# Conditioning rows of a transformer layer: added one transfer step later, in written order, from three buffers; later shift and scale columns by one-column products

## The chip, the cores and the metric

The kernel runs on one core of a Trainium2 chip. The metric is the time on the device in microseconds, the median of several runs. TensorE (PE) does the matrix products, VectorE (DVE) and ScalarE (ACT) the elementwise work, GpSimd (POOL) a little of it, and SyncE (SP) issues nearly all transfers into on-chip memory, in order. Each engine works through its own queue of instructions in a fixed order and waits, where it must, for another engine or a transfer.

## The reference

One layer, 256 tokens of 2048 features, all in fp32. A vector `c` gives nine vectors of 2048 by one large matrix, `w_ada` (2048 x 18432, 151 MB): a shift, a scale and a gate for each of three parts.

```python
ada = (silu(c) @ w_ada + b_ada)
sh1, sc1, g1, sh2, sc2, g2, sh3, sc3, g3 = split(ada, 9)
h = swiglu(layernorm(x) * (1 + sc1) + sh1, ffn1_w_in, ffn1_w_out)
x = layernorm(ALPHA * x + 0.5 * (1 + g1) * h, ln1_g, ln1_b)
h = token_mixer(layernorm(x) * (1 + sc2) + sh2, ...)      # 8 attention heads, 4 mLSTM heads, w_out
x = layernorm(ALPHA * x + (1 + g2) * h, ln2_g, ln2_b)
h = swiglu(layernorm(x) * (1 + sc3) + sh3, ffn2_w_in, ffn2_w_out)
x = layernorm(ALPHA * x + 0.5 * (1 + g3) * h, ln3_g, ln3_b)
```

## The kernel before

**Products.** Each fp32 operand is split into a rounded high part and the rest, and a product is three matmuls: high by high (L355), low by high (L356), high by low (L357). Weights come in tiles of 1 MB by SP's queue (`raw_...`, three buffers); ScalarE writes the high part (`hi_...`, L145), VectorE subtracts it to get the low part (`lo_...`, L146). In names, `s` and `f1i` are FFN1's input product, `f1o` its output product, `mo`, `fv`, `mv` parts of the mixer's input product, `mxo` its output product, `fh` and `gf` (`gu`) the beginning of FFN2's input product, `f2i` the rest of it, `f2o` its output product. `hT` is a hidden row of the FFN, `hh` and `hl` its two parts, `o_f` and `o_mx` the output sums.

**The conditioning vectors.** They are not computed on TensorE as a product with a single row. A block of 128 rows of `w_ada` by 1024 columns (512 KB, `ar...`) is transferred, and VectorE multiplies it by one scalar for each partition and adds it to a sum (`acc`, L158 for the first, L160 for the other fifteen of a sum). The 128 partitions are then added up by a product with ones:
- The first shift and scale (`first_ada`, L691) take products of one column each: 128 columns of the sum as weights, a column of ones as moving operand. What comes out already lies one feature to a partition, as `scsh` needs it.
- All later sums are split, and a matrix of ones gives the sum in all partitions (`bc`, L173). For a gate that is the form in which it is used (L213). For a shift or scale the diagonal has to be picked out: a multiplication with the identity (`dg`, L191), a reduction (L193), and the bias (L195).

**The order of this work.** Everything after the first pair is one generator, `ada_queue`. The loops over weight tiles call `pump(n)`, which goes on by `n` steps (rates `R_F` to `R_B` for the stages); one step issues a row's transfer and its add, in two buffers. `need(n)` drains the queue up to part `n` where its result is used:

```python
    def need(n):
        while parts_done[0] < n and next(ada_left["g"], 0) != 0:
            owed[0] = 0
```

The framework's scheduler may move instructions on an engine within what the data allow; so a written add can end up earlier or later on VectorE than its neighbours in the code. `out_proj` keeps unfinished additions to the residual in a list and lets `catch_up(n)` write `n` of them for each weight tile.

Of the kernel before, what the change touches and what calls it, by code (L numbers as in the profile page):

```python
# [47 lines left out]
def layer_kernel(  # L48
# [41 lines left out]
    tri = ap.tile([P, 2 * P], F32, tag="ahi", name="tri")  # L90
# [9 lines left out]
    crow = ap.tile([KD, P], F32, tag="alo", name="crow")  # L100
# [15 lines left out]
    def load_bcol():  # L116
        brow = ap.tile([72, 2, P], F32, tag="ahi", name="brow")
# [38 lines left out]
    def ada_acc(acc, raw, k):  # L156
        if k == 0:
            V.tensor_scalar_mul(acc, raw, csil[:, k:k + 1])  # L158
        else:
            V.scalar_tensor_tensor(out=acc, in0=raw, scalar=csil[:, k:k + 1], in1=acc,  # L160
                                   op0=ALU.mult, op1=ALU.add)


    def ada_split(acc, tag):
        ahi = ap.tile([P, 512], F32R, tag="ahi", name=f"ahi{tag}")
        alo = ap.tile([P, 512], F32R, tag="alo", name=f"alo{tag}")
        split(acc, ahi, alo)
        return ahi, alo

    def ada_sum(parts, tag):  # L170
        bc = aux_tile(f"bc{tag}")
        for i in range(2):
            PE.matmul(bc, onesr, parts[i], start=i == 0, stop=i == 1)  # L173
        return bc

    def ada_pair(v, js):
        for j in js:
            src = pair_cols(v, j)
            acc = ap.tile([P, 2, 512], F32, tag="acc", name=f"acc{v}_{j}")
            for k in range(KD):  # L180
                raw = ap.tile([P, 2, 512], F32, tag="araw", bufs=2, name=f"ar{v}_{j}_{k}")
                SP.dma_start(raw, src[k * P:(k + 1) * P])
                ada_acc(acc, raw, k)
                yield
            for i in range(2):
                parts = ada_split(acc[:, i, :], f"{v}_{j}_{i}")
                for _ in range(2):
                    yield PAUSE
                bc = ada_sum(parts, f"{v}_{j}_{i}")
                dg = ap.tile([P, 4, P], F32, tag="alo", name=f"dg{v}_{j}_{i}")  # L190
                V.tensor_tensor(out=dg, in0=bc.rearrange("p (a b) -> p a b", b=P),  # L191
                                in1=ident.unsqueeze(1).to_broadcast([P, 4, P]), op=ALU.mult)
                V.tensor_reduce(out=scsh[:, v + i, j * 4:(j + 1) * 4], in_=dg, axis=AX.X, op=ALU.add)  # L193
            cs = scsh[:, v:v + 2, j * 4:(j + 1) * 4]
            V.tensor_tensor(out=cs, in0=cs, in1=bcol[:, v:v + 2, j * 4:(j + 1) * 4], op=ALU.add)  # L195

    def ada_gate(v, s):
        for j in range(2):
            c0 = v * D + j * 1024
            acc = ap.tile([P, 1024], F32, tag="acc", name=f"acc{v}_{j}")  # L200
            for k in range(KD):
                raw = ap.tile([P, 1024], F32, tag="araw", bufs=2, name=f"ar{v}_{j}_{k}")
                SP.dma_start(raw, w_ada[0, k * P:(k + 1) * P, c0:c0 + 1024])
                ada_acc(acc, raw, k)
                yield
            G_.dma_start(gate[:, j * 1024:(j + 1) * 1024], b_ada[0:1, c0:c0 + 1024].to_broadcast([P, 1024]))
            for i in range(2):
                parts = ada_split(acc[:, i * 512:(i + 1) * 512], f"{v}_{j}_{i}")
                for _ in range(2):
                    yield PAUSE  # L210
                bc = ada_sum(parts, f"{v}_{j}_{i}")
                gs = gate[:, j * 1024 + i * 512:j * 1024 + (i + 1) * 512]
                V.scalar_tensor_tensor(out=gs, in0=bc, scalar=1.0, in1=gs, op0=ALU.add, op1=ALU.add)  # L213
                if s != 1.0:
                    V.tensor_scalar_mul(gs, gs, s)

    ada_left = {}
    PAUSE = 1

    def ada_queue(*parts):  # L220
        def gen():
            for p in parts:
                yield from p
                parts_done[0] += 1
                yield PAUSE
        ada_left["g"] = gen()

    parts_done = [0]
    owed = [0]

    def pump(n):
        owed[0] += n
        while owed[0] >= 1:
            if next(ada_left["g"], 0) is PAUSE:
                break
            owed[0] -= 1


    def need(n):
        while parts_done[0] < n and next(ada_left["g"], 0) != 0:  # L240
            owed[0] = 0


# [141 lines left out]
    def out_proj(w, rows, nk, tag, npump, finish, before=None, turn=0, nheld=3, spare=None):  # L385
# [11 lines left out]
        for width in (1024, 512, 512):  # L397
# [40 lines left out]
            for i in range(nu):  # L438
# [19 lines left out]
                if not lastg and i == nu - 1:  # L458

                    late += [add_up(a, bs=(b,)) for b in range(nb) for a in range(2)]  # L460
                    products(0, held)
                    catch_up(2)
                    products(1, held)
                else:
                    catch_up(2)
                if not lastg or i < nu - 4:
                    npump()
            if lastg:
                catch_up(99)
                finish(last_products, add_up, st)  # L470
            else:
                col += width
# [50 lines left out]
    def boundary(products, add_up, st, lgb, v, tag, xT, entry, nk):  # L523
# [3 lines left out]
        sq = ap.tile([P, 1024], F32, tag="araw", bufs=2, name=f"sq_{tag}")  # L527
# [83 lines left out]
    def cols_1024(raws, xs, split_, load, ps, xT, npump, u0, u1):  # L611
# [6 lines left out]
        for u in range(u0 + len(raws), u1):  # L618
            for k, hi, lo in split_.get(u) or load(u):
# [18 lines left out]
    R_F, R_IN, R_OUT, R_MX, R_A, R_B = 1.25, 1.2, 1, 1.42, .9, .6  # L638
# [14 lines left out]
    def first_ada(j, ws=iter(())):  # L653
# [5 lines left out]
        for kk in range(8):  # L659
            if kk % 3 == 2:  # L660
                raws = []
                for h in range(2):
                    k = 2 * kk + h
                    raw = ap.tile([P, 2, 512], F32, tag="araw", bufs=2, name=f"ar0_{j}_{k}")
# [106 lines left out]
    with tc.manual_schedule(engines={mybir.EngineType.DVE, mybir.EngineType.Activation}):  # L771
        next(fa)
    ada_queue(ada_gate(2, 0.5), ada_pair(3, range(4)), ada_pair(6, range(2)), ada_gate(5, 1.0),
              ada_pair(6, range(2, 3)), ada_pair(6, range(3, 4)), ada_gate(8, 0.5))
    for j in range(4):
        fa = first_ada(j + 1) if j < 3 else load_mixer_smalls()
        for i in range(NS):
            first_in(j, i, ws if i + j == 0 else first_w(j, i))
            for _ in range(i not in (4, 9, 11)):
                next(fa, 0)  # L780
            if j == 3 and i > 2:
# [9 lines left out]
    need(1)  # L791
# [14 lines left out]
    def finish1(products, add_up, st):  # L806
        need(2)
# [376 lines left out]

    def before(k):
        until([f"row{i}" for i in (k, k + 1)])
        if k == 2:
            need(4)
# [80 lines left out]
    for j in range(2, 10):  # L1269
# [12 lines left out]
    for _ in mb:  # L1282
        pass
    gups = {(a, g): mm_tile(f"gf{g}{a}") for a in range(2) for g in range(2)}
    cols_1024([], {}, {}, gu_load, gups, xT, at(R_B), 4, 8)
# [23 lines left out]
    need(7)  # L1309
# [42 lines left out]
```

## Time and profile before

| | us |
|---|---|
| three runs | 1976.5, 1969.3, 1975.67; median 1975.67 |
| the profiled execution | 1967.35 |
| its span from first to last instruction | 1965.6 |
| TensorE busy | 1900.2 |
| VectorE busy | 1486.1 |
| ScalarE busy | 944.3 |
| mean granted clock of TensorE | 0.995 |

The profiled execution is 1.75 us longer than its span. Times inside it are counted from the span's start. In a row of a timeline stand the start, the duration, the engine, the line, the operation with its output and inputs, and in brackets how long the engine idled before it and what ended that. In a row of waits stand the total, the number and the longest. Matmuls overlap, so their cost is the distance from start to start, and the printed duration is longer. In a row of windows the columns behind the engines' busy times are the granted clock, the share of the transfer engines and GB/s.

### The profile page before, as it was taken

To read this page: it belongs to the slowest core of one execution; us is meant where nothing else is said; L and a number is where in the kernel's file an instruction comes from. 1 tells how busy PE (TensorE), PEld (TensorE's weight loads), DVE (VectorE), ACT (ScalarE), POOL (GpSimd) and SP (SyncE) were. 2 spreads that over 40 slices of the span, in tenths; PEclk is the share of its full clock that TensorE was granted. 3 is DMA by queue.
4 is the path that set the end of the run, shared out by engine and by line. 5 is a ranking of instruction groups with operands and counts; after the bars stand their busy time and mean duration, and the time that the engine had idled before them with its cause. 6 is when DMAs were issued, how large, how long until landed. Compare 5 with 4: busy or idle time off the path is not lost.

```text
span 1965.6 us, 32416 instructions
## 1 busy us (share of the span) xinstructions
PE 1900.2 (97%) x13201; PEld 1736.7 (88%) x13201; DVE 1486.1 (76%) x1827; ACT 944.3 (48%) x1328; POOL 19.6 (1%) x34
## 2 busy tenths in 40 slices
PE   3999999999999999999999999999999999999997
PEld 3999999999988888588999876899999999988886
DVE  7788888777778898678888687778756645555776
ACT  2544354443444554645755543555444444444552
POOL 0000000000000000000000000000000000000000
PEclk9999999999999999999999999999999999999998
DMA  9999878989989785589888784898757855655552
GB/s 335 333 326 315 309 234 294 310 291 303 317 297 310 269 292 199 174 302 298 268 299 287 266 276 147 293 297 296 260 194 254 278 194 187 236 191 192 193 193 86
DMA packets 301822, 510.91 MB, mean 260 GB/s; under 512 B 10819, under 2 KB 158691, under 8 KB 300649
## 3 DMA queue, kind: packets, MB, share of 16 engines
q1 hardware_dynamic: 300808, 505.70, 76.5%
q0 software_dynamic: 864, 3.15, 0.5%
q8 instruction: 103, 1.69, 0.4%
q14 instruction: 47, 0.38, 0.1%
HBM read 506.71 MB, written 2.10 MB: 259 GB/s over the span
## 4 chain that ended last, share of the span: by engine, by line
PE 77%; DMA 9%; DVE 9%; ACT 2%; issue 2%; POOL 0%; SPq 0%; DVEq 0%; ACTq 0%; POOLq 0%
PE o_f L355 8%; PE o_f L357 8%; PE o_f L356 8%; PE gu_f L355 7%; PE gu_f L357 7%; PE gu_f L356 7%; DMA ar<-in_w_ada_dram 5%; PE s L357 3%; PE s L355 3%; PE s L356 3%; DVE acc L160 2%; PE pr_f L356 2%; PE pr_f L355 2%; PE pr_f L357 2%; PE fs L355 1%
## 5 line engine op out<-in xcount | busy, mean ns | idle before, releaser
L160 DVE SCALAR_TENSOR_TENSOR acc<-ar,csil,acc 128x1024 f32<-128x1024 f32 x242 | 307.7, 1272 | 106.7 <-DMA ar<-in_w_ada_dram 105.3
L355 PE MATMUL s<-xhi_f,hi_s 128*128 128x256 f32 x768 | 213.8, 279 | 0.8 <-ACT hi_s L145 0.6
L357 PE MATMUL s<-xhi_f,lo_s 128*128 128x256 f32 x768 | 213.1, 278 | 0.6 <-DVE lo_s L146 0.5
L356 PE MATMUL s<-xlo_f,hi_s 128*128 128x256 f32 x768 | 213.4, 278 | 0.0
L357 PE MATMUL gu_f<-xhi_f,lo_f2i 128*128 128x256 f32 x768 | 212.0, 276 | 0.0
L355 PE MATMUL gu_f<-xhi_f,hi_f2i 128*128 128x256 f32 x768 | 212.0, 276 | 0.0
L356 PE MATMUL gu_f<-xlo_f,hi_f2i 128*128 128x256 f32 x768 | 212.0, 276 | 0.0
L146 DVE TENSOR_TENSOR lo_f2i<-raw_f2i,hi_f2i 128x1024 fp32r<-128x1024 f32 x96 | 116.8, 1223 | 89.5 <-ACT hi_f2i L145 89.5
L355 PE MATMUL gu_f<-xhi_f,hi_f1i 128*128 128x256 f32 x640 | 176.8, 276 | 0.2 <-DVE hT L740 0.2
L357 PE MATMUL gu_f<-xhi_f,lo_f1i 128*128 128x256 f32 x640 | 176.7, 276 | 0.0
L356 PE MATMUL gu_f<-xlo_f,hi_f1i 128*128 128x256 f32 x640 | 176.7, 276 | 0.0
L145 ACT CAST hi_f2i<-raw_f2i 128x1024 fp32r<-128x1024 f32 x96 | 100.4, 1049 | 133.7 <-PE gu_f L356 112.4
L355 PEld LDWEIGHTS s<-xhi_f,hi_s 128*128 128x128 f32 x768 | 145.1, 189 | 1.1 <-ACT hi_s L145 0.7
L357 PEld LDWEIGHTS s<-xhi_f,lo_s 128*128 128x128 f32 x768 | 144.9, 189 | 1.1 <-DVE lo_s L146 1.1
L356 PEld LDWEIGHTS s<-xlo_f,hi_s 128*128 128x128 f32 x768 | 145.2, 189 | 0.3 <-DVE xlo_f L297 0.3
L356 PEld LDWEIGHTS gu_f<-xlo_f,hi_f2i 128*128 128x128 f32 x768 | 144.1, 188 | 0.2
L355 PEld LDWEIGHTS gu_f<-xhi_f,hi_f2i 128*128 128x128 f32 x768 | 144.1, 188 | 0.2
L145 ACT CAST hi_s<-raw_s 128x1024 fp32r<-128x1024 f32 x96 | 97.3, 1050 | 97.5 <-DMA raw_s<-in_ffn_w_in_dram 56.6
L357 PEld LDWEIGHTS gu_f<-xhi_f,lo_f2i 128*128 128x128 f32 x768 | 144.1, 188 | 0.0
L146 DVE TENSOR_TENSOR lo_f2o<-raw_f2o,hi_f2o 128x1024 fp32r<-128x1024 f32 x88 | 107.7, 1224 | 44.9 <-ACT hi_f2o L145 44.8
L355 PE MATMUL o_f<-hi_f2o,hh 128*128 128x512 f32 (+1 forms) x368 | 139.4, 379 | 0.0
L357 PE MATMUL o_f<-hi_f2o,hl 128*128 128x512 f32 (+1 forms) x368 | 138.7, 377 | 0.0
(451 smaller groups left out, 5342.0 us busy)
## 6 DMA issues: line engine op xcount, KB each, us to landing
ar<-in_w_ada_dram SPq DMA_DIRECT2D x288, 512.0 KB, 5.7
raw_s<-in_ffn_w_in_dram SPq DMA_DIRECT2D x48, 1024.0 KB, 6.0
raw_f2i<-in_ffn_w_in_dram SPq DMA_DIRECT2D x48, 1024.0 KB, 5.1
raw_f1o<-in_ffn_w_out_dram SPq DMA_DIRECT2D x44, 1024.0 KB, 6.9
raw_f2o<-in_ffn_w_out_dram SPq DMA_DIRECT2D x44, 1024.0 KB, 5.1
raw_f1i<-in_ffn_w_in_dram SPq DMA_DIRECT2D x40, 1024.0 KB, 7.7
raw_mxo<-in_w_out_dram SPq DMA_DIRECT2D x16, 1024.0 KB, 6.8
raw_fh<-in_ffn_w_in_dram SPq DMA_DIRECT2D x16, 1024.0 KB, 7.5
```

The source lines that it names most:

```text
L145: S.copy(hi, src)
L146: V.tensor_tensor(out=lo, in0=src, in1=hi.bitcast(F32), op=ALU.subtract)
L160: V.scalar_tensor_tensor(out=acc, in0=raw, scalar=csil[:, k:k + 1], in1=acc, op0=ALU.mult, op1=ALU.add)
L355: PE.matmul(o, ah, bh, start=start, stop=False)
L356: PE.matmul(o, ah, bl, start=False, stop=False)
L357: return PE.matmul(o, al, bh, start=False, stop=stop)
```

## The change

- **Rows.** Transfers are issued by `ada_rows` into three buffers and noted in `landing`. The next call of `pump` or `need` writes their adds first (`add_landed`); at most two rows wait at a time. `keep_in_program_order` forbids the scheduler to move an add past its neighbours in the written order. At most three steps can be owed.
- **Sums.** What a sum needs after its last row (`columns`) is a generator of its own, which goes on by one step at each `pump`, beside the next sum's rows. A later shift and scale takes eight one-column products of the unsplit sum (L192) and one addition of the bias; the split, `bc`, `dg` and the reduction are gone. A gate's sum is split in one piece of 1024 columns instead of two of 512.
- **Places.** `R_OUT` is 1.1 instead of 1, `R_A` 1.2 instead of 0.9. `need` counts smaller parts and stands elsewhere: in the mixer's output product before units 8 and 12, in `fh` at step 7. The modulation of chunk 3 for FFN2, with its `need`, moves from `fh` (step 9) into `gf` between two weight tiles (`last_features`). `out_proj` catches up three pieces instead of two for the wide columns and none in the last group before its end. The first stage issues weights before it goes on with the first ada sums.

The core of the diff:

```diff
-    def ada_pair(v, js):
-        for j in js:
-            ...
-            acc = ap.tile([P, 2, 512], F32, tag="acc", name=f"acc{v}_{j}")
-            for k in range(KD):
-                raw = ap.tile([P, 2, 512], F32, tag="araw", bufs=2, name=f"ar{v}_{j}_{k}")
-                SP.dma_start(raw, src[k * P:(k + 1) * P])
-                ada_acc(acc, raw, k)
-                yield
-            for i in range(2):
-                parts = ada_split(acc[:, i, :], f"{v}_{j}_{i}")
-                for _ in range(2):
-                    yield PAUSE
-                bc = ada_sum(parts, f"{v}_{j}_{i}")
-                dg = ap.tile([P, 4, P], F32, tag="alo", name=f"dg{v}_{j}_{i}")
-                V.tensor_tensor(out=dg, in0=bc..., in1=ident..., op=ALU.mult)
-                V.tensor_reduce(out=scsh[:, v + i, j * 4:(j + 1) * 4], in_=dg, axis=AX.X, op=ALU.add)
+    def ada_acc(acc, raw, k):
+        ...
+        tc.keep_in_program_order(ins)
+
+    def ada_rows(acc, src, tag):
+        for k in range(KD):
+            raw = ap.tile([P, 1024], F32, tag="araw", bufs=3, name=f"ar{tag}_{k}")
+            SP.dma_start(raw.rearrange("p (v n) -> p v n", v=2), src[k * P:(k + 1) * P])
+            landing.append((acc, raw, k))
+            yield PAUSE if k == KD - 1 else None
+
+    def ada_pair(v, j):
+        acc = ap.tile([P, 1024], F32, tag="acc", name=f"acc{tag}")
+        yield from ada_rows(acc, pair_cols(v, j), tag)
+
+        def columns():
+            yield
+            cp = aux_tile(f"ac{tag}")[:, :8]
+            for i in range(8):
+                PE.matmul(cp[:, i:i + 1], acc[:, i * P:(i + 1) * P], ones[:, 0:1], start=True, stop=True)
+            yield
+            V.tensor_tensor(out=scsh[:, v:v + 2, js], in0=cp..., in1=bcol[:, v:v + 2, js], op=ALU.add)
+        yield columns()
+
     def pump(n):
-        owed[0] += n
-        while owed[0] >= 1:
-            if next(ada_left["g"], 0) is PAUSE:
-                break
-            owed[0] -= 1
+        add_landed()
+        end_columns()
+        ada["owed"] = min(ada["owed"] + n, 3)
+        while ada["owed"] >= 1 and len(landing) < 2 and not (ada["ends"] and ada["beside"]):
+            got = next_row()
+            ...
@@ out_proj
-                else:
+                elif nu > 4:
                     catch_up(2)
+                elif not lastg:
+                    catch_up(3)
...
-    R_F, R_IN, R_OUT, R_MX, R_A, R_B = 1.25, 1.2, 1, 1.42, .9, .6
+    R_F, R_IN, R_OUT, R_MX, R_A, R_B = 1.25, 1.2, 1.1, 1.42, 1.2, .6
...
-        if j in (7, 9):
-            need(5 if j == 7 else 6)
-            mb = modulate_both(6, 2 if j == 7 else 3, mr2, xT)
+        if j == 7:
+            need(11)
+            mb = modulate_both(6, 2, mr2, xT)
...
+    def last_features(u):
+        if u == 5:
+            need(12)
+            mb.append(modulate_both(6, 3, mr2, xT))
```

Three places show how the instructions stand now.

VectorE, the beginning of FFN1's output product; `acc_1` is a sum of the second shift and scale (its rows `ar_1_...`), `hT` the last rows that this product needs first. Before:

```order
L160 SCALAR_TENSOR_TENSOR acc_1_5912<-ar_1_8_6119,csil,acc_1_5912 128x1024
L160 SCALAR_TENSOR_TENSOR acc_1_5912<-ar_1_9_6122,csil,acc_1_5912 128x1024
L146 TENSOR_TENSOR lo_f1o_11_6271<-raw_f1o_1_6252,hi_f1o_11_6270 128x1024
L146 TENSOR_TENSOR lo_f1o_20_6296<-raw_f1o_2_6293,hi_f1o_20_6295 128x1024
L160 SCALAR_TENSOR_TENSOR acc_1_5912<-ar_1_10_6183,csil,acc_1_5912 128x1024
L380 TENSOR_TENSOR hT_3_111<-sg_f_0_6186,gu_f_0_5937 128x256
L160 SCALAR_TENSOR_TENSOR acc_1_5912<-ar_1_11_6245,csil,acc_1_5912 128x1024
L380 TENSOR_TENSOR hT_3_111<-sg_f_1_6189,gu_f_1_5938 128x256
```

After the change, the same place:

```order
L160 SCALAR_TENSOR_TENSOR acc_1_5709<-ar_1_10_6223,csil,acc_1_5709 128x1024
L146 TENSOR_TENSOR lo_f1o_20_6273<-raw_f1o_2_6270,hi_f1o_20_6272 128x1024
L402 TENSOR_TENSOR hT_3_111<-sg_f_0_6162,gu_f_0_5913 128x256
L146 TENSOR_TENSOR lo_f1o_21_6289<-raw_f1o_2_6270,hi_f1o_21_6288 128x1024
L402 TENSOR_TENSOR hT_3_111<-sg_f_1_6165,gu_f_1_5914 128x256
L146 TENSOR_TENSOR hl_6226<-hT_0_108,hh_6225 128x512
L146 TENSOR_TENSOR hl_6267<-hT_0_108,hh_6266 128x512
L160 SCALAR_TENSOR_TENSOR acc_1_5709<-ar_1_11_6264,csil,acc_1_5709 128x1024
```

The add of row 10 went ahead of `lo_f1o_20`, and that of row 11 behind both `hT` and two `hl`.

VectorE, the last part of the mixer's output product: low parts of its weights (`lo_mxo`) and the pieces that add the product to the residual (`o_mx` times gate, `res`, and its statistics `st_mx`). Before:

```order
L146 TENSOR_TENSOR lo_mxo_20_12252<-raw_mxo_2_12249,hi_mxo_20_12251 128x1024
L435 BN_STATS st_mx_11638<-res 128x6
L146 TENSOR_TENSOR lo_mxo_21_12256<-raw_mxo_2_12249,hi_mxo_21_12255 128x1024
L431 TENSOR_TENSOR o_mx_12057<-o_mx_12057,gate 128x512
L146 TENSOR_TENSOR lo_mxo_30_12264<-raw_mxo_3_12261,hi_mxo_30_12263 128x1024
L433 SCALAR_TENSOR_TENSOR res<-res,o_mx_12057 128x512
L146 TENSOR_TENSOR lo_mxo_31_12268<-raw_mxo_3_12261,hi_mxo_31_12267 128x1024
L435 BN_STATS st_mx_11637<-res 128x6
L431 TENSOR_TENSOR o_mx_12058<-o_mx_12058,gate 128x512
L146 TENSOR_TENSOR lo_mxo_00_12276<-raw_mxo_0_12273,hi_mxo_00_12275 128x1024
```

After the change:

```order
L146 TENSOR_TENSOR lo_mxo_20_12174<-raw_mxo_2_12171,hi_mxo_20_12173 128x1024
L453 TENSOR_TENSOR o_mx_11977<-o_mx_11977,gate 128x512
L160 SCALAR_TENSOR_TENSOR acc_2_11516<-ar_2_15_12100,csil,acc_2_11516 128x1024
L146 TENSOR_TENSOR lo_mxo_21_12178<-raw_mxo_2_12171,hi_mxo_21_12177 128x1024
L146 TENSOR_TENSOR lo_mxo_30_12184<-raw_mxo_3_12181,hi_mxo_30_12183 128x1024
L146 TENSOR_TENSOR lo_mxo_31_12188<-raw_mxo_3_12181,hi_mxo_31_12187 128x1024
L146 TENSOR_TENSOR lo_mxo_00_12194<-raw_mxo_0_12191,hi_mxo_00_12193 128x1024
L146 TENSOR_TENSOR lo_mxo_01_12198<-raw_mxo_0_12191,hi_mxo_01_12197 128x1024
L455 SCALAR_TENSOR_TENSOR res<-res,o_mx_11977 128x512
L453 TENSOR_TENSOR o_mx_11978<-o_mx_11978,gate 128x512
```

The low parts stand together now and the pieces of the residual follow them, while the last add of the sum `acc_2`, which lay ahead of this place before, stands among them.

SP, the transfers of the mixer's input weights `fv` and `mv` with ada rows between them. Before:

```order
L339 DMA raw_fv_0_8709<-in_w_in_dram 128x4x520
L182 DMA ar_0_2_8576<-in_w_ada_dram 128x2x512
L182 DMA ar_0_3_8579<-in_w_ada_dram 128x2x512
L339 DMA raw_fv_1_8778<-in_w_in_dram 128x4x520
L182 DMA ar_0_4_8616<-in_w_ada_dram 128x2x512
L182 DMA ar_0_5_8653<-in_w_ada_dram 128x2x512
L339 DMA raw_fv_2_8847<-in_w_in_dram 128x4x520
```

After the change:

```order
L361 DMA raw_fv_0_8673<-in_w_in_dram 128x4x520
L168 DMA ar_0_9_8544<-in_w_ada_dram 128x2x512
L168 DMA ar_0_10_8582<-in_w_ada_dram 128x2x512
L361 DMA raw_fv_1_8743<-in_w_in_dram 128x4x520
L168 DMA ar_0_11_8619<-in_w_ada_dram 128x2x512
L168 DMA ar_0_12_8621<-in_w_ada_dram 128x2x512
L168 DMA ar_0_13_8741<-in_w_ada_dram 128x2x512
L361 DMA raw_fv_2_8812<-in_w_in_dram 128x4x520
```

Three rows instead of two stand ahead of `raw_fv_2`; the queue goes on with two rows, `raw_fv_3`, one row, `raw_mv_0` and `raw_mv_1`, where two rows stood ahead of each before. Later, five rows stand in one piece between `raw_mxo_0` and `raw_mxo_1`.

More of the change, by code (lines that the diff above doesn't have):

```diff
@@ L157, in ada_acc @@
         if k == 0:
-            V.tensor_scalar_mul(acc, raw, csil[:, k:k + 1])
+            ins = V.tensor_scalar_mul(acc, raw, csil[:, k:k + 1])
         else:
[L160 to L168, printed above, removed]
@@ L217, in layer_kernel @@
[L217 to L229, printed above, removed]
-    def pump(n):
-        owed[0] += n
-        while owed[0] >= 1:
-            if next(ada_left["g"], 0) is PAUSE:
-                break
-            owed[0] -= 1
-    def need(n):
-        while parts_done[0] < n and next(ada_left["g"], 0) != 0:
-            owed[0] = 0
+            ins = V.scalar_tensor_tensor(out=acc, in0=raw, scalar=csil[:, k:k + 1], in1=acc,
+                                         op0=ALU.mult, op1=ALU.add)
@@ new lines, in layer_kernel, with add_landed, end_columns, next_row @@
+    PAUSE, STARTED, ENDED = 1, 2, 3
+    ada = {"left": [], "rows": None, "ends": None, "beside": 0, "done": 0, "owed": 0}
+    landing = []
+    def add_landed():
+        while landing:
+            ada_acc(*landing.pop(0))
+    def end_columns():
+        if ada["ends"] and next(ada["ends"], 0) == 0:
+            ada["ends"] = None
+            ada["done"] += 1
+    def next_row():
+        if not ada["rows"]:
+            if not ada["left"]:
+                return ENDED
+            ada["rows"] = ada["left"].pop(0)
+        got = next(ada["rows"])
+        if got in (None, PAUSE):
+            return got
+        ada.update(ends=got, rows=None, beside=0)
+        next(got)
+        return STARTED
@@ L790, in layer_kernel @@
     gap(lnp, 320, "gap_h")
-    need(1)
+    need(2)
     W = w_in[0]
@@ L1308, in layer_kernel @@
     ffn_in(W2, xT, hT, 10, "f2", at(R_B))
-    need(7)
+    need(14)
     xp.release()
```

108 lines of the change are left out of this document (66 added, 42 removed).

## The prediction

> **What bounds the kernel now.** I read the page's head first, then the waits of TensorE, then the timeline of TensorE and of VectorE around each wait, and last the groups by form for the prices.
>
> ```profile
> span 1965.6 us, 32416 instructions
> PE 1900.2 (97%) x13201; PEld 1736.7 (88%) x13201; DVE 1486.1 (76%) x1827; ACT 944.3 (48%) x1328; POOL 19.6 (1%) x34
> ...
> 400.00:500.00 100.00, 100.00 (x880) 99.82 (x879) 71.96 (x73) 40.81 (x49) 0.00 (x0) 1.00 0.92 304
> ```
>
> TensorE works for 97% of the span; in the window from 400 to 500 us it never idles, and its 880 matmuls of 256 columns give the pitch that I use below, 0.11 us. An edit can gain only where TensorE idles or runs at a lower clock, and every matmul that is added lengthens the span unless it falls into such a hole. VectorE has 480 us to spare on average, so work taken from it counts only where TensorE waits for it. The next view lists what TensorE waited for (total us, times, longest).
>
> ```profile
> PE cp L691 <- DVE gate L160: 14.3, 1, 14.3
> PE o_mx L356 <- DVE lo_mxo L146: 3.6, 4, 1.2
> PE cp L691 <- DVE scsh L693: 3.1, 2, 2.6
> PE bc L173 <- ACT ahi L145: 3.0, 1, 3.0
> ...
> PE b_fv L355 <- ACT og L1144: 1.9, 1, 1.9
> PE o_f L355 <- DVE hT L380: 1.8, 1, 1.8
> PE b_mv L355 <- ACT yF L943: 1.4, 1, 1.4
> PE b_mv L355 <- ACT yM L1004: 1.3, 1, 1.3
> ...
> PE bc L173 <- DVE alo L146: 0.5, 1, 0.5
> ```
>
> The first row is the start, which lasts until the first ada rows have come; the change leaves its transfers as they are. The rows on `o_mx`, `scsh`, `ahi`, `o_f` and `alo` are 12.0 us, and all lie where ada rows are added. The cause shows in this row of the page: VectorE stood 105.3 us in front of an add, waiting for the row's transfer.
>
> ```profile
> L160 DVE SCALAR_TENSOR_TENSOR acc<-ar,csil,acc 128x1024 f32<-128x1024 f32 x242 | 307.7, 1272 | 106.7 <-DMA ar<-in_w_ada_dram 105.3
> ```
>
> **What the change takes away.** Adds now come one step after their transfer was issued, so what stood behind a waiting add on VectorE goes first. Four places, with starts on TensorE and VectorE:
>
> ```profile
> 174.23 0.28 PE L357 MATMUL s<-xhi_f,lo_s 128*128 128x256 f32 x1
> 177.11 0.61 PE L691 MATMUL cp<-trir,gate 128*128 128x1 f32 x4 [2.60 <-DVE scsh L693]
> 174.50 1.28 DVE L160 SCALAR_TENSOR_TENSOR acc<-ar,csil,acc 128x1024 f32<-128x1024 f32 x1 [3.40 <-DMA ar<-in_w_ada_dram]
> ```
>
> (1) At 174 us VectorE stood 3.40 us in front of the first stored sum's add, and the four shift and scale adds lay behind it. In the new order they lie ahead of it. Gone: 177.11 − 174.23 − one pitch of 0.11 = 2.8 us, and 0.5 us of the same kind at 104 us (the other of the two waits). Together 3.3.
>
> ```profile
> 539.65 1.28 DVE L160 SCALAR_TENSOR_TENSOR acc<-ar,csil,acc 128x1024 f32<-128x1024 f32 x1 [0.30 <-DMA ar<-in_w_ada_dram]
> 539.12 0.40 PE L357 MATMUL o_f<-hi_f1o,h 128*128 128x512 f32 x1
> 541.32 0.60 PE L355 MATMUL o_f<-hi_f1o,h 128*128 128x512 f32 x1 [1.81 <-DVE hT L380]
> 545.08 0.40 PE L355 MATMUL o_f<-hi_f1o,h 128*128 128x512 f32 x1
> ```
>
> (2) At 539 us the `hT` that the next products need lies behind this add, which waited itself and came late. TensorE loses 541.32 − 539.12 − 0.23 = 2.0 us, and then its next nine matmuls need 545.08 − 541.32 = 3.76 us where nine pitches of 0.23 are 2.1, since the clock had dropped: 1.7 more. The new order has `hT` right after `lo_f1o_20`, the adds behind both `hT`. Gone: 3.7.
>
> The wait here was 1.8 us, and still the slow clock followed. [...]
>
> ```profile
> 1165.56 1.28 DVE L160 SCALAR_TENSOR_TENSOR acc<-ar,csil,acc 128x1024 f32<-128x1024 f32 x1 [2.27 <-DMA ar<-in_w_ada_dram]
> 1191.18 0.38 PE L355 MATMUL o_mx<-hi_mxo,yhi 128*128 128x256 f32 x1
> 1192.76 0.39 PE L356 MATMUL o_mx<-lo_mxo,yhi 128*128 128x256 f32 x1 [1.20 <-DVE lo_mxo L146]
> 1193.45 0.34 PE L355 MATMUL o_mx<-hi_mxo,yhi 128*128 128x256 f32 x1
> 1197.01 0.28 PE L355 MATMUL o_mx<-hi_mxo,yh 128*128 128x256 f32 x1
> 1150.00:1200.00 50.00, 46.26 (x221) 38.00 (x221) 40.08 (x45) 14.89 (x17) 0.61 (x1) 0.97 0.82 275
> ```
>
> (3) The end of the mixer's output product. VectorE waits in front of adds (2.27 us the longest) and is late with the last four low parts. The four waits are 3.6 us, but with the restart behind each one start-to-start loss is larger: the last is 1192.76 − 1191.18 − 0.12 = 1.46 for a wait of 1.20. By that ratio of 1.22 they cost 4.4 us. Then 15 pitches take 1197.01 − 1193.45 = 3.56 us instead of 1.76. Gone: 4.4 + 1.8 = 6.2. The window's last columns (clock 0.97, DMA 0.82, 275 GB/s) say that the transfers are not the limit there. In the new order the low parts lie ahead of the residual's last pieces.
>
> ```profile
> 1321.26 0.28 PE L357 MATMUL fh<-xhi_f,lo_fh 128*128 128x256 f32 x1
> 1324.54 0.50 PE L173 MATMUL bc<-ahi,trir 128*128 128x512 f32 x1 [3.00 <-ACT ahi L145]
> ```
>
> (4) Here `need(6)` drains a pair, and TensorE waits for the split of its sum: 1324.54 − 1321.26 − 0.11 = 3.2, and 0.5 for `alo`. In the new kernel the pair is finished a stage later, beside other products, and its sum is not split. Gone: 3.7.
>
> Together 3.3 + 3.7 + 6.2 + 3.7 = 16.9 us. I add 0.5 for waits under half a microsecond that VectorE's lighter load should shorten (not shown row by row): 17.4.
>
> **What it costs.** Columns by one-column products. They are in the trace at the first pair, and the old way beside them:
>
> ```profile
> 102.55 0.50 PE L691 MATMUL cp<-trir,acc 128*128 128x1 f32 x4
> 102.91 0.58 PE L691 MATMUL cq<-trir,acc 128*128 128x1 f32 x4
> 103.36 0.36 PE L355 MATMUL s<-xhi_f,hi_s 128*128 128x256 f32 x1
> 103.56 0.28 PE L356 MATMUL s<-xlo_f,hi_s 128*128 128x256 f32 x1
> 1319.87 0.39 PE L173 MATMUL bc<-ahi,trir 128*128 128x512 f32 x1
> 1320.10 0.39 PE L173 MATMUL bc<-alo,trir 128*128 128x512 f32 x1
> 1320.33 0.28 PE L355 MATMUL fh<-xhi_f,hi_fh 128*128 128x256 f32 x1
> ```
>
> Four products (eight records) hold TensorE from 102.55 to 103.36, 0.81 us, and the next matmul's pitch is 0.20 instead of 0.11: 0.90. A pair needs eight: 1.79. The old way takes 1320.33 − 1319.87 = 0.46 for each half, 0.92 for a pair. Eight pairs: 8 × (1.79 − 0.92) = **6.9 us dearer**. Nothing hides it, as TensorE is the bound; between 6 and 8.
>
> VectorE is relieved. Per pair half it loses a low part, a diagonal multiply and a reduction:
>
> ```profile
> L191 DVE TENSOR_TENSOR dg<-bc,ident x16: 680/683/692, 504.3 to 1327.6; 128x512 f32<-128x512 f32 x16
> L193 DVE TENSOR_REDUCE scsh<-dg x16: 675/678/687, 506.1 to 1328.9; 128x4 f32<-128x512 f32 x16
> L146 DVE TENSOR_TENSOR alo<-acc,ahi x28: 675/684/693, 338.1 to 1641.1; 128x512 fp32r<-128x512 f32 x28
> ```
>
> 16 × (0.68 + 0.68 + 0.68) = 33 us, and ScalarE 16 casts. I cost that at nothing and count no gain beyond the 17.4: both engines have room, and what VectorE gave back at TensorE's waits is in (1) to (4).
>
> Chunk 3's modulation moves from `fh` into `gf` between two weight tiles, with 12 products of the remaining part as cover (12 × 0.113 = 1.4 us). ScalarE may stand at one cast of a weight, 1.05 us, when its work is wanted:
>
> ```profile
> L145 ACT CAST hi_f2i<-raw_f2i 128x1024 fp32r<-128x1024 f32 x96 | 100.4, 1049 | 133.7 <-PE gu_f L356 112.4
> ```
>
> Between 0 (the cover is enough) and 1.05; I take 0.4. At the start two adds go behind a small vector operation that waits for GpSimd; TensorE waits for this chain (first row of the waits). Between 0 and 1.3 (one add of the row above); I take 0.4. The gates' split in one piece of 1024 instead of two of 512, the third buffer, and SP's order of transfers move the same bytes: 0. At 840 to 895 us (`b_fv`, `b_mv`), where TensorE waited for ScalarE behind late weights, the new order puts other numbers of ada rows ahead of the weights: counted from `raw_fv_0`, `raw_fv_2` comes behind five rows instead of four, `raw_mv_1` behind eight instead of ten. Between −6.5 (the three rows' 4.6 us of waits with their restarts and one slow stretch go) and +3 (one row of 512 KB more, 1.9 us at the 275 GB/s above, and a restart at half clock); I take 0.
>
> **Sum.** −17.4 + 6.9 + 0.4 + 0.4 = **−9.7 us**. The profiled execution took 1967.35 us, its span being 1965.6, and becomes 1957.7. It was the fastest shown; the median is 1975.67, so I expect 1966.
>
> **Rivals.**
>
> *More goes (B).* The waits at 840 to 895 us vanish as well: −9.7 − 6.5 = −16.2, so 1959.5. For it: the weights from `raw_mv_1` on lie behind two to four rows fewer. Against it: the longest of these waits, `b_fv`, comes before that point.
>
> *The waits move (C).* An add one step late still stands in a queue that is served in order. If half of the 17.4 us, 8.7, turns up elsewhere, for example at weights behind three to five ada rows in one bunch on SP's queue (five between `raw_mxo_0` and `raw_mxo_1`, 512 KB each at 275 GB/s, 1.9 us apiece): −8.7 + 7.7 = −1.0, so 1974.7.
>
> *It does not do what it says (E).* A row lands 5.7 us after its issue in the median:
>
> ```profile
> ar<-in_w_ada_dram SPq DMA_DIRECT2D x288, 512.0 KB, 5.7
> ```
>
> If a step is shorter than that, an add one step behind still waits, the 105 us remain and so do TensorE's waits: +7.7, so 1983.4, within 0.5%.
>
> *Slower (D).* Adds may no longer pass one another or give way, as their order is fixed. TensorE lost 16.9 us for 106.7 us of waits at adds, 0.16 for each. If they grow, the loss grows with them; with the columns' 7.7 it is over +9.9 us from 120 us of waits on. At 160 us: 25.5 − 16.9 + 7.7 = +16.3, so 1992. For it: rows are bunched more than before; against it: each add has a step more to land and there is a third buffer.
>
> **How the numbers follow.** A, the sum as worked, 0.50; its own range is 1961 to 1971 by the bounds of the columns, the modulation and the weights. B 0.17, C 0.15, E 0.05, D 0.13. About 0.5% (9.9 us, 1965.8) is what a measurement of this kernel can tell from no change. A lies on this bound, and I give it 0.27 faster and 0.23 same. Faster 0.27 + 0.17 = 0.44; same 0.23 + 0.15 + 0.05 = 0.43; slower 0.13. The range runs from 1955 (B with 4 us more) to 1981, which leaves out D and the upper end of E.
>
> **What would show it.** Right: the row of waits of `cp` for `scsh` is gone, `o_f` no longer waits for `hT`, `o_mx` for `lo_mxo` has under 1 us, and no `ahi` row is left; the granted clock in the windows at 500 and 1150 is 1.00; the group of ada adds has clearly less than 106.7 us of idle time before it; 128 records of one-column products `ac` take 14 us. Wrong: the idle time before the adds stays over 100 us, new rows of TensorE waiting for `lo` tiles or for `ac`, or weights late at `raw_mxo`. If the adds no longer wait and the time is still the same, the columns cost more than 1.8 us a pair or the transfers decide.

## The result, and the profile after

The changed kernel takes 1955.66 us (median of 13 runs, 1952.71 to 1958.49), the kernel before in the same comparison 1970.5 us. The ratio is 0.9927, 95% interval 0.9913 to 0.9941: 0.73% or 14 us faster. The forecast was 9.7 us. The profiled execution's span went from 1965.6 to 1951.1 us. First the page: its head, and the group of ada adds (busy, mean ns of one, idle before it).

```profile
span 1951.1 us, 32572 instructions
PE 1898.5 (97%) x13297; PEld 1741.2 (89%) x13297; DVE 1461.1 (75%) x1773; ACT 939.9 (48%) x1306; POOL 19.0 (1%) x34
...
L160 DVE SCALAR_TENSOR_TENSOR acc<-ar,csil,acc 128x1024 f32<-128x1024 f32 x242 | 307.0, 1269 | 24.6 <-DMA ar<-in_w_ada_dram 23.8
```

VectorE waited 106.7 us in front of adds, now 24.6. TensorE's busy time fell by 1.7 us although it has 6.9 us more to do. Slow stretches count as busy, and by the clock records of the traces (from which the granted clock is taken) the kernel before had three of 3.41 us at half clock (at 541.6, 845.4 and 1193.5 us), which cost 5.1 us; the changed kernel has none before the last 10 us of its span. The other 3.5 us are not assigned to rows. The waits of TensorE behind the start:

```profile
PE ytp L1159 <- DVE gate L214: 2.4, 1, 2.4
PE b_fv L377 <- ACT og L1173: 1.7, 1, 1.7
...
PE o_mx L378 <- DVE lo_mxo L146: 0.2, 1, 0.2
```

The rows on `scsh`, `hT`, `ahi` and `alo` are gone, and `lo_mxo` fell from 3.6 to 0.2. Also gone are both rows on `b_mv`, for which I had counted nothing. New is `ytp`. The windows around places (2), (3) and (4):

```profile
500.00:550.00 50.00, 50.00 (x367) 46.90 (x367) 42.67 (x44) 21.98 (x28) 0.00 (x0) 1.00 0.93 339
1150.00:1200.00 50.00, 49.61 (x250) 41.31 (x248) 44.24 (x65) 15.76 (x21) 2.88 (x4) 1.00 0.66 221
1300.00:1350.00 50.00, 49.93 (x341) 45.52 (x340) 35.86 (x47) 29.11 (x50) 0.00 (x0) 1.00 0.79 264
```

The granted clock (third column from the end) is 1.00 in each, where it was 0.97 in the windows from 500 and from 1150 before; TensorE works nearly all the time. At places (1) and (2), at 173 and 533 us, the urgent work on VectorE now stands ahead of the adds:

```profile
173.18 0.15 DVE L720 TENSOR_TENSOR scsh<-cp,bcol 128x2 f32<-128x2 f32 x1
175.39 1.28 DVE L160 SCALAR_TENSOR_TENSOR acc<-ar,csil,acc 128x1024 f32<-128x1024 f32 x1
...
533.46 0.42 DVE L402 TENSOR_TENSOR hT<-sg_f,gu_f 128x256 f32<-128x256 f32 x1 [0.60 <-ACT sg_f L401]
537.08 1.28 DVE L160 SCALAR_TENSOR_TENSOR acc<-ar,csil,acc 128x1024 f32<-128x1024 f32 x1
```

Stage by stage, from the first matmul of one group of names to that of the next, in us:

| from to | before | after | difference |
|---|---|---|---|
| start to `s` | 37.8 | 38.5 | +0.7 |
| `s` to `gu_f` | 278.4 | 273.3 | −5.1 |
| `gu_f` to `o_f` | 221.0 | 221.4 | +0.4 |
| `o_f` to `mo` | 250.5 | 249.1 | −1.4 |
| `mo` to `ytp` | 244.7 | 243.0 | −1.7 |
| `ytp` to `ge` | 180.3 | 175.3 | −5.0 |
| `ge` to `fh` | 29.1 | 30.7 | +1.6 |
| `fh` to `gf` | 94.8 | 89.9 | −4.9 |
| `gf` to the end | 629.0 | 629.9 | +0.9 |

### The profile page after: what moved, and what is told of

The parts are those of the page before. It is cut to its first block, busy times and chain, and to the rows that moved or that the text cites. A ratio compares the mean times of both kernels' runs of the same rounds, so it can differ in the third digit from the quotient of the medians.

```text
span 1951.1 us, 32572 instructions
## 1 busy us (share of the span) xinstructions
PE 1898.5 (97%) x13297; PEld 1741.2 (89%) x13297; DVE 1461.1 (75%) x1773; ACT 939.9 (48%) x1306; POOL 19.0 (1%) x34
## 4 chain that ended last, share of the span: by engine, by line
PE 92%; DVE 5%; DMA 1%; issue 1%; ACT 1%; POOL 0%; DVEq 0%; SPq 0%; POOLq 0%; ACTq 0%
PE gu_f L379 8%; PE gu_f L377 8%; PE gu_f L378 8%; PE o_f L377 8%; PE o_f L379 8%; PE o_f L378 8%; PE s L377 5%; PE s L379 5%; PE s L378 5%; PE pr_f L378 2%; PE pr_f L377 2%; PE pr_f L379 2%; PE fh L377 2%; PE fh L378 1%; PE fh L379 1%; PE fs L378 1%
## 5 line engine op out<-in xcount | busy, mean ns | idle before, releaser
L160 DVE SCALAR_TENSOR_TENSOR acc<-ar,csil,acc 128x1024 f32<-128x1024 f32 x242 | 307.0, 1269 | 24.6 <-DMA ar<-in_w_ada_dram 23.8
L145 ACT CAST hh<-hT 128x512 fp32r<-128x512 f32 x128 | 78.6, 621 | 138.6 <-PE o_f L378 136.9
```

The costliest lines, as they stand in the source:

```text
L145: S.copy(hi, src)
L160: ins = V.scalar_tensor_tensor(out=acc, in0=raw, scalar=csil[:, k:k + 1], in1=acc, op0=ALU.mult, op1=ALU.add)
```

## The experiments

All ratios are to the kernel before, timed on the same chip. "Idle" is VectorE's idle time in front of the adds from each page, and the span is that of the profiled execution. One execution of a kernel differs from the next by some us (the changed kernel's 13 runs go from 1952.71 to 1958.49), so times are compared by the ratios, and a profile is read for its waits.

| kernel | ratio | 95% interval | span | idle |
|---|---|---|---|---|
| before | 1 | | 1965.6 | 106.7 |
| after | 0.9927 | 0.9913 to 0.9941 | 1951.1 | 24.6 |
| e1 old columns | 0.9907 | 0.9888 to 0.9926 | 1949.7 | 37.8 |
| e2 columns alone | 1.0043 | 1.0026 to 1.0061 | 1977.5 | 112.0 |
| e3 no step | 0.9896 | 0.9875 to 0.9917 | 1950.9 | 16.9 |
| e4 free order | 1.0011 | 0.9994 to 1.0028 | 1969.4 | 85.7 |
| e5 order alone | 1.0113 | 1.0078 to 1.0147 | 1987.5 | 92.9 |
| e6 no step, old columns | 0.9895 | 0.9866 to 0.9924 | 1950.6 | 29.7 |
| e7 two buffers | 0.9961 | 0.9942 to 0.9980 | 1965.9 | 72.2 |
| e8 old rates | 0.9900 | 0.9869 to 0.9930 | 1950.2 | 18.6 |
| e9 no step, two buffers | 0.9965 | 0.9952 to 0.9979 | 1961.0 | 72.9 |
| e10 no step, free order | 1.0016 | 1.0002 to 1.0030 | 1968.1 | 90.3 |
| e11 no step, old rates | 0.9905 | 0.9887 to 0.9923 | 1948.8 | 15.1 |
| e12 old first stage | 1.0062 | 1.0040 to 1.0085 | 1981.7 | 25.6 |

**The step (e3).**

```diff
-            landing.append((acc, raw, k))
+            ada_acc(acc, raw, k)
```

> The changed kernel, but each add is written directly behind its transfer's issue, no longer one step later; written order, three buffers, places and columns stay. My theory: the step between is what took the adds out of the way; the idle time before adds goes from 24.6 back to 70 us or more, half or all of the 17 us of the four places come back, ratio 0.997 to 1.002. Rival: three buffers and the other places of the needs are what counts; then it is within 3 us of the changed kernel, ratio 0.992 to 0.995.

The rival won, and at 0.9896 the kernel came out below even the rival's range. The page's row:

```profile
L160 DVE SCALAR_TENSOR_TENSOR acc<-ar,csil,acc 128x1024 f32<-128x1024 f32 x242 | 307.7, 1272 | 16.9 <-DMA ar<-in_w_ada_dram 15.8
```

An add written right behind its transfer waits less, not more, and the time is no worse (the intervals of e3 and after just overlap). The step that gives the change its name isn't needed.

**The order (e4, and e10 without the step).**

```diff
-        tc.keep_in_program_order(ins)
```

> The changed kernel without the rule that adds keep their written place, so that the scheduler may move them again. My theory: an add written one step late keeps most of its lateness; within 4 us of the changed kernel, ratio 0.991 to 0.995, idle time before adds below 50 us. Rival: the scheduler pulls the adds forward to where they waited before; idle time before adds over 80 us, ratio 0.998 or more.

Again the rival. The page of e4, and the waits of its TensorE:

```profile
L160 DVE SCALAR_TENSOR_TENSOR acc<-ar,csil,acc 128x1024 f32<-128x1024 f32 x242 | 308.1, 1274 | 85.7 <-DMA ar<-in_w_ada_dram 84.5
```

```profile
PE ytp L1158 <- DVE gate L213: 5.6, 1, 5.6
PE cp L717 <- DVE scsh L719: 2.9, 1, 2.9
...
PE gu_f L378 <- DVE lo_f1i L146: 2.3, 4, 0.8
```

The wait for `scsh` is back at 2.9 us, and the whole gain is gone. Without the rule the scheduler again puts an add, which waits 3.56 us for its row, ahead of the urgent `scsh`:

```profile
174.15 1.28 DVE L160 SCALAR_TENSOR_TENSOR acc<-ar,csil,acc 128x1024 f32<-128x1024 f32 x1 [3.56 <-DMA ar<-in_w_ada_dram]
...
176.55 0.16 DVE L719 TENSOR_TENSOR scsh<-cp,bcol 128x2 f32<-128x2 f32 x1
```

The other rows of e4, `ytp` and `gu_f`, are not places of the prediction: waits have also moved. By the clock records, 6.83 us at half clock begin at 177.2 us, right behind the wait for `scsh`, and again at 1040.7 us, within the one at `ytp`.

> The changed kernel without the step and without the rule of written order: three buffers, new columns and new places alone. Theory: the scheduler again puts adds ahead of work that is ready sooner on the chip; idle time before adds 80 to 120 us, ratio 0.999 to 1.005, no better than with the step (1.001). Rival: three buffers alone are enough once the step is away; idle time below 50 us, ratio below 0.996.

Without the step the same: 90.3 us of idle time, ratio 1.0016. So three buffers, new columns and new places together give no gain in time without the written order.

**The order alone (e5).** In the kernel before, `ada_acc` gets the rule and nothing else is changed.

> The kernel before, with the one rule that an add keeps its written place on VectorE; two buffers, no step between, old columns, old places of the needs. My first theory (the step between counts) fell with the run that took the step away. New theory: the scheduler had put adds ahead of work whose data were there sooner than the row; the rule alone then takes the idle time before adds from 107 to below 60 us and gives half or more of the gain, ratio 0.990 to 0.996. Rival: an add written directly behind its own transfer, in two buffers, waits all the same; idle time over 80 us, ratio 0.998 or more.

A miss for the new theory, with the rival's idle time (92.9 us): 1.1% slower, the slowest of all. The waits of TensorE:

```profile
PE s L358 <- DVE lo_s L146: 10.2, 10, 2.4
PE s L356 <- ACT hi_s L145: 6.3, 7, 2.2
```

16 us of them lie in the first stage (`s`), where the kernel before had 0.5 for `lo_s`. Two things could be wrong there, the buffers or the places.

**Buffers (e7, and e9 without the step).** `bufs=3` becomes `bufs=2` for the rows.

> The changed kernel with two row buffers instead of three. Theory: with one step of delay two rows are on their way, so the third buffer only spares SP a wait for an add; rows and the weights behind them come a little later, 0 to 5 us slower than the changed kernel, ratio 0.993 to 0.995. Rival: SP's queue stands behind each row until an add is done and weights come late at many places, ratio 0.997 or more.

> The changed kernel without the step between transfer and add, and with two row buffers instead of three; written order kept. Theory after the runs so far: SP's queue runs ahead of VectorE until a buffer is missing, so the number of buffers sets how long a row has to land, and the step in the written code sets it only where SP is held up. Then this kernel is like the one with the step and two buffers (idle time before adds 72 us): 60 to 110 us, ratio 0.995 to 1.004. Rival: the step is what helps with two buffers (the kernel before with written order alone became 1.1% slower); then idle time over 120 us and ratio 1.006 or more. A second rival: buffers don't matter without the step; idle time under 40 us and ratio below 0.993.

Idle times of 72.2 and 72.9 us, ratios 0.9961 and 0.9965: e7 between its two ranges, e9 as the theory had it. With two buffers the step is worth nothing as well. Against the same kernel with three buffers, about half of the gain is lost in e7 and two thirds in e9, most of it (6.7 and 6.4 us by the spans) in the stage from `o_f` to `mo`. There the wait at `hT` is back, in e9 with 2.0 us, in e7 with twice what it was before the change:

```profile
PE o_f L377 <- DVE hT L402: 3.7, 1, 3.7
```

So it is the third buffer that gives rows time to land: SP's queue runs ahead of VectorE until a buffer is missing (in the changed kernel it stood 304.6 us in front of row transfers, L168, until an add had ended), and the written step does not hold it back. The traces show this directly. From the issue of a row's transfer to the start of its add, over the 224 rows of the later sums, the mean time is 9.6 and 9.2 us with two buffers (e7, e9), with the step or without, and 14.8 and 14.2 us with three (after, e3). The kernel before has 9.7, e5 10.3. With three buffers and free order (e4, e10) it is 11.7 and 11.6, so more than half of what the buffer gives is gone. Four buffers were not tried.

**Place by place.** TensorE's waits at the four places of the prediction, in us in total, 0 where the page of waits has no row:

| kernel | (1) `scsh` | (2) `hT` | (3) `lo_mxo` | (4) `ahi`, `alo` |
|---|---|---|---|---|
| before | 3.1 | 1.8 | 3.6 | 3.5 |
| after | 0 | 0 | 0.2 | 0 |
| e4, e10 free order | 2.9, 2.4 | 0 | 0 | 0 |
| e5 order alone | 0 | 0.9 | 4.6 | 0 |
| e7, e9 two buffers | 0, 0.7 | 3.7, 2.0 | 0.9 | 0 |

In e5 `alo` has 2.1 us, but at 790 us, not at place (4). The places don't have one cause. (1) comes back without the written order. (2) stays away without it and comes back with two buffers, and with 3.0 us in e6 below, where the old columns lie in the rows' three buffers. (3) stays away without the order, nearly so with two buffers, and stays as it was with the order alone; it goes with the new places in `out_proj` (e8 below, with the old rates, has 0.2), and no run took back one of these alone. (4) is gone in every run. What free order loses, it loses at (1) and at new waits: `lo_f1i` 2.3 and 4.0 us, `ytp` 5.6 and 6.1 us in e4 and e10, with a slow stretch of 6.83 us at `ytp` in both.

**The first stage (e12).**

```diff
-            w = list(ws if i + j == 0 else first_w(j, i))
-            for _ in range(i not in (4, 9, 10)):
+            first_in(j, i, ws if i + j == 0 else first_w(j, i))
+            for _ in range(i not in (4, 9, 11)):
                 next(fa, 0)
-            first_in(j, i, w)
```

> The changed kernel with the old order of writing in its first stage (a block's products first, then a step of the next first ada sum; the steps left out at 4, 9 and 11). Written order alone made the kernel before 1.1% slower, and 16 us of its waits lay in this stage, TensorE waiting for high and low parts of its weights. Theory: with the rule of written order this stage needs its adds written where they now stand; with the old places the waits of about 16 us between 44 and 316 us come back, ratio 0.998 to 1.004. Rival: those waits came from the two buffers; then this kernel is within 3 us of the changed one, ratio 0.991 to 0.995.

1.0062, more than the theory's range: these lines are worth 27 us beside the rule of written order, twice the change's whole gain. `gu_f` begins at 341.9 us instead of 311.8, and from there to `gf` the two kernels take the same 1010 us. A window of 100 us in this stage (the changed kernel's below it), TensorE's waits between 44 and 316 us, and the one row of ScalarE that stands out:

```profile
144.00:244.00 100.00, 87.64 (x706) 85.23 (x707) 76.53 (x88) 33.92 (x40) 0.73 (x1) 0.95 0.73 257
```

```profile
144.00:244.00 100.00, 100.00 (x882) 99.82 (x881) 90.46 (x108) 43.95 (x54) 0.73 (x1) 1.00 0.91 314
```

```profile
PE s L377 <- ACT hi_s L145: 9.4, 6, 3.1
PE s L379 <- DVE lo_s L146: 8.2, 8, 2.6
```

```profile
145.72 1.99 ACT L145 CAST hi_s<-raw_s 128x1024 fp32r<-128x1024 f32 x2 [11.14 <-DMA raw_s<-in_ffn_w_in_dram]
```

TensorE does 706 matmuls where the changed kernel does 882, the transfer engines are busy 0.73 of the time instead of 0.91, and ScalarE waits 11 us for a weight tile. The waits (17.6 us) and five slow stretches that cost 1.7 us each (the granted clock is 0.95 and 0.97 in e12's windows from 144 and from 244 us, 1.00 in both in the changed kernel) are 26 of the 27 us. No engine is overloaded. In this stage most ada rows lie in the weights' own buffers (`tag="raw"` in `first_ada`), so an add that stands late in VectorE's queue keeps a buffer from the next weights. SP's own waits in the stage show it: in front of weight transfers (L361) it stood 52.8 us until an add had ended, in the changed kernel 16.7 us. First e12, then the changed kernel:

```profile
SPq L361 <- DVE acc L160: 32.0, 9, 9.0
SPq L361 <- DVE gate L160: 20.8, 5, 7.0
```

```profile
SPq L361 <- DVE acc L160: 13.0, 6, 3.3
SPq L361 <- DVE gate L160: 3.7, 2, 2.2
```

That this is the whole reason is not shown; no run gave those rows buffers of their own. The length of this stage (`s` to `gu_f`) in the other runs answers the question left by e5. With the rule and the old lines it takes 299.6 and 303.4 us (e5 with two buffers, e12 with three), with the rule and the new lines 273.3 and 273.7 (after, e3) and with two buffers 274.7 and 274.2 (e7, e9). Without the rule it takes 278.4 with the old lines (before), 280.6 and 277.1 with the new ones (e4, e10). So e5's loss there came from the places and not from the buffers, and the new lines are not shown to be worth anything without the rule.

**The columns (e1, e2).** In e1 the changed kernel gets back the split, the product with ones, `dg` and the reduction; in e2 the kernel before gets the one-column products alone.

> The changed kernel, but later shift and scale columns come as before (split, product with a matrix of ones, diagonal, reduction). My theory: one-column products cost TensorE 8 x (1.79 - 0.92) = 6.9 us that nothing hides, and VectorE's relief of 33 us is worth nothing; so this kernel is 5 to 7 us faster than the changed one, a ratio to the kernel before of 0.989 to 0.991, and TensorE shows no new waits. Rival: the relief is what removed TensorE's waits; then rows of TensorE waiting for low parts, for the split or for the reduction come back, and the ratio is 0.993 or more.

The price on TensorE was right to the digit. The start of eight products and of the next matmul in the changed kernel:

```profile
498.74 1.84 PE L192 MATMUL ac<-trir,acc 128*128 128x1 f32 x16
500.44 0.36 PE L377 MATMUL gu_f<-xhi_f,hi_f1i 128*128 128x256 f32 x1
500.64 0.28 PE L378 MATMUL gu_f<-xlo_f,hi_f1i 128*128 128x256 f32 x1
```

1.70 us, and 0.09 in the next pitch: 1.79 for a pair. But e1 is only 1.4 us shorter in span, and 3.9 us by the ratios, not 6.9. It has new waits of TensorE for VectorE:

```profile
PE fs L384 <- DVE lo_fs L146: 1.6, 1, 1.6
...
PE o_f L383 <- DVE lo_f1o L146: 0.7, 2, 0.5
```

All of TensorE's waits after 44 us come to 10.6 us in e1 and 7.4 in the changed kernel, and e1 has a slow stretch at 1127 us. But 2.1 us of e1's waits lie in the first stage, ahead of the first of these columns, and that stage took 2.4 us longer, although VectorE had the same 319 instructions in the same order as in the changed kernel. That is a difference of two executions, not of the columns. Without it the spans say what the ratios say: the old columns' load on VectorE costs about 3 of the 6.9 us that they save. Part of that may come from the buffers, since in e1 the split parts and `dg` lie in the rows' three buffers (`araw`), which they do not in the kernel before; no run tells the two apart. The intervals of e1 and after overlap, so neither way of getting columns is shown to be better.

> The kernel before, with the later shift and scale columns from one-column products and nothing else changed. My theory: TensorE has 6.9 us more work, and only the wait behind the drained pair at 1321 us (3.7 us) becomes shorter, as no split follows the last add; the adds still wait some 100 us for their rows. So 3 to 7 us slower than before, ratio 1.002 to 1.004. Rival: VectorE's relief removes the waits at the four places; then 5 us or more faster, ratio below 0.997.

Slower by 0.43%, just above my range; the rows for `ahi` and `alo` are gone and the others are still there:

```profile
PE o_f L355 <- DVE hT L380: 4.7, 1, 4.7
PE cp L691 <- DVE scsh L693: 4.6, 2, 3.1
PE o_mx L356 <- DVE lo_mxo L146: 3.3, 4, 1.4
```

Place (4) needs no later drain then, only a sum that isn't split. At the other three places a lighter VectorE did not help. That the rows on `scsh` and `hT` are longer than before is not shown to come from the edit. Up to `gu_f`, VectorE, ScalarE and SP have the same instructions in the same order as in the kernel before, and yet this execution took 283.4 us for the first stage instead of 278.4; its clock records have 10.2 us at half clock there, a loss of 5.1 us.

**Both edits (e6), the rates (e8), and both of those (e11).**

> The changed kernel without the step between transfer and add and with the old columns (split, diagonal, reduction): two edits that each ran alone. Theory: the two are independent; TensorE has 6.9 us less to do than with one-column products, and new waits for VectorE take 3 to 5 us of that, as they did with the step; ratio 0.987 to 0.990. Rival: without the step VectorE has less room for the old columns, more waits come, ratio 0.991 or more.

Near the upper end of the theory's range, and the rival's shape: 1950.6 us of span against 1950.9 with one-column products. VectorE is late for `hT` by 3.0 us again. The columns are a draw here too.

> The changed kernel with the old rates of two stages (1 instead of 1.1 and 0.9 instead of 1.2), so fewer rows in FFN1's output product and in the beginning of FFN2's. Theory: the rates move work between stages that have room; within 3 us of the changed kernel, ratio 0.991 to 0.994. Rival: rows are left over at the needs, which then drain them at once; TensorE waits there for the sums, ratio 0.995 or more.

> The changed kernel without the step and with the old two rates: two edits that each alone gave 0.990. Theory: each left TensorE with few waits between 40 us and the end, and the waits that are left at 780 to 845 us and 1198 to 1224 us are the same in both; so they don't add up, ratio 0.988 to 0.992. Rival: they take away different waits (the one at 1025 us for a gate's addition is gone in both), ratio 0.987 or less.

Rates: no loss by going back, 0.9900, which is even better than the theory's range, so the new ones are not shown to help. The two do not add up (0.9905), as expected. e3, e6, e8 and e11 lie between 0.9895 and 0.9905, their intervals overlap with one another and with that of the changed kernel; the shortest span, 1948.8, is e11's.

## Why the prediction was right, and where its reasons were not

The sign was right, and the time lies in the range, but at its very end: 1955.66 us, where the range began at 1955. Of the 10.3 us between it and the 1966 that I expected, 5.2 are the kernel before, whose median was 1970.5 in the comparison and not 1975.67; the rest is a gain of 14.8 instead of 9.7 us. The own range of the sum, 1961 to 1971, was missed, and rival B with its 1959.5 came nearer. That a sum with the wrong cause gave the right sign is partly luck: the same edit held the written order, the third buffer and the new places. Point by point:

- **The four places.** Sized well and all gone: 3.3, 3.7, 6.2 and 3.7 us. The stage of (1) became 5.1 us shorter; that of (2) 1.4, with 2.6 us of dearer columns in it; that of (3) 5.0, with `ytp`'s new 2.4 us in it; that of (4) 4.9, of which about 0.9 are eight transposes that moved with the modulation into the next stage.
- **Why they go.** Wrong. I put it down to the step between transfer and add. e3 and e9 show that the step does nothing, with three buffers or two; e4 and e10 that without the written order the gain is gone, by (1) and by new waits elsewhere; e7 and e9 that the third buffer, which I had put at 0, is what removes (2) and is half of the gain or more; e5 and e12 that the order costs more than it gives unless the first stage is written anew. I had read the first stage's edit as two adds that move, at 0.4 us.
- **The columns.** About 6.9 us dearer on TensorE as counted (8 × 0.87 is 7.0), but the relief of VectorE, for which I counted no gain, was mis-sized: by e1 it is worth about 3 us, and by e6 against e3 about all of the 6.9.
- **840 to 895 us.** Taken as 0; the two `b_mv` waits (2.7 us and their restarts) and the slow stretch behind `b_fv` went, which is 4.7 of the 6.5 us of rival B. The wait at `b_fv` stayed, 1.7 us for 1.9.
- **A wait not foreseen.** `ytp`, 2.4 us. VectorE stood in front of an add, and a gate's addition behind it kept a sum's place from TensorE:

```profile
1025.24 1.28 DVE L160 SCALAR_TENSOR_TENSOR acc<-ar,csil,acc 128x1024 f32<-128x1024 f32 x1 [3.59 <-DMA ar<-in_w_ada_dram]
1026.44 1.22 DVE L146 TENSOR_TENSOR lo_f1a<-raw_f1a,hi_f1a 128x1024 fp32r<-128x1024 f32 x1
1027.58 1.28 DVE L214 SCALAR_TENSOR_TENSOR gate<-bc,gate 128x512 f32<-128x512 f32 x2
```

  It is the mechanism of the old waits, at a new place. In e3, e8 and e11 it does not occur; in e3 the gate's addition at 1024.82 stands ahead of the add at 1026.03.
- **The modulation in `gf`.** No wait, where 0.4 was taken.
- **Rival D.** Its mechanism, that a fixed order turns against the kernel, came true in e5 and e12; but the quantity I tied it to, idle time in front of adds, does not show it: e12 has 25.6 us, as little as the changed kernel, and is 1.4% slower than it.

From the forecast 9.7 to the spans' 14.5: plus 4.7 for `b_mv` with restarts (3.0) and the slow stretch (1.7), plus 1.3 by which the first stage got shorter beyond what was counted, plus 0.4 for the modulation, less 2.4 for `ytp` and 0.3 at the start. That is 13.4; 1.1 us stay unassigned, less than what two executions of the same instructions differed by in e1's first stage (2.4).

## What to carry to other kernels

How long a transfer had to land was set here by the number of buffers (9.2 and 9.6 us from issue to add with two, 14.2 and 14.8 with three), not by how far apart issue and use were written (the larger of each two is with the step): the issuing queue ran ahead until a buffer was missing. If a scheduler moves early-ready work in front of urgent work, pinning the order is a strong lever in both directions: undo it alone, and apply it alone, before giving the credit to anything else. Follow each wait through these runs, not only the time: here four waits that looked alike went for different reasons. When work is taken off an engine that isn't the bound, look at whether the bound waits for it at places before calling it worthless.

## What the runs showed of the hardware

A drop of the clock did not go by the length of one wait in these runs. In the kernel before, the clock was halved right behind a wait of 1.8 us: the matmul after it starts at 541.32 us, the half clock at 541.6, and the granted clock from 541 to 546 us is 0.66. In the run without step and with old columns the wait at the same place was 3.0 us:

```profile
537.46 0.50 PE L382 MATMUL o_f<-hi_f1o,h 128*128 128x512 f32 x1 [3.00 <-DVE hT L407]
537.80 0.39 PE L383 MATMUL o_f<-lo_f1o,h 128*128 128x512 f32 x1
538.03 0.40 PE L384 MATMUL o_f<-hi_f1o,h 128*128 128x512 f32 x1
...
538.73 0.63 PE L384 MATMUL o_f<-hi_f1o,h 128*128 128x512 f32 x1
539.16 0.63 PE L382 MATMUL o_f<-hi_f1o,h 128*128 128x512 f32 x1
```

The first matmuls behind it run at the full pitch of 0.23 us, and the slow ones (0.43) begin 1.3 us later. The wait of 2.4 us at 1025 us in the changed kernel was followed by no slow stretch at all: the granted clock from 1020 to 1040 us is 1.00. A wait thus cost here between little more than its length (2.6 us for 2.4, at 1025 us in the changed kernel: 3.0 us from start to start across it, 0.4 to the next start) and its length plus 1.9 us (3.7 for 1.8, at 541 us before).

Apart from the end of the run, the slow stretches in the clock records of the kernel before are 3.41 us long, all three, and begin at 541.6, 845.4 and 1193.5 us. No run shows what decides whether a wait is followed by one.
